# One weight sum of the Strassen-like gate/up sets, written in place

## The chip, the cores and the metric

The kernel runs on one core of a Trainium2 chip. The metric is the device time of one execution, in microseconds, lower is better. Before the change it is 1257.70 us, the median of three runs (1257.69 to 1257.84). One further execution was taken with the hardware profiler; everything below that is called a row of the profile or of the trace comes from that execution.

## The reference

The reference is a decoder trunk of two layers on 256 tokens of width 1024 in float32. Each layer adds, one after the other, half a SwiGLU feed-forward network (FFN), a token mixer (differential attention in layer 0, a Mamba-2 mixer in layer 1), a cross-attention into 256 memory tokens, and half of a second FFN:

```
def swiglu(h, w_gate, w_up, w_down):
    return (jax.nn.silu(h @ w_gate) * (h @ w_up)) @ w_down
...
    h = h + 0.5 * swiglu(rmsnorm(h, ffn1_norm[i]), ffn1_w_gate[i], ffn1_w_up[i], ffn1_w_down[i])
```

There are so four FFNs, and each has a gate and an up matrix of 1024 x 2816 and a down matrix of 2816 x 1024. What matters here is `h @ w_gate` and `h @ w_up`.

## The kernel before, in words

**Three products for one.** To reach float32 accuracy every operand is cut into two fp32r parts, high and low, and every product is made as three TensorE products: high x high, high x low, low x high (`mm3`, L261 to L264). The left operand is kept in its two parts. The weights come from memory in float32 and are cut on the chip: a granule (`Gran`, L205) is a piece of 128 x 1024 elements of a weight buffer; its `split` casts the high part on ACT (L224, tile `whi`) and then subtracts on DVE to get the low part (L225, tile `wlo`). There are four `whi` and four `wlo` buffers (pool `hp`), so the cast of a granule has to wait until TensorE is done with the granule four places ahead of it.

**Seven products for eight.** For blocks of 512 hidden columns, gate and up are made together by a Strassen-like scheme (`seven`, L361) that takes seven half-size products where the plain way takes eight. The weights of one such set are four tiles of 512 x 512: B11 and B21 (the upper and lower half of the rows of the up matrix), B12 and B22 (the same of the gate matrix). Beside products with B11, B22 and B21 themselves, the scheme needs products with four sums: x1 = B11 + B12, x2 = x1 + B22, x3 = B12 + B22, and x4 = x2 + B21. Signs sit on the left operand. There are 15 such sets: blocks 2, 3 and 4 of the first FFN and blocks 1 to 4 of the other three. Cross-attention calls `seven` twice more, with another order of the products.

**How the sums are made.** `Sum.load` (L186 to L203) makes a sum when its first granule is cut. With `into` unset it takes a weight buffer of its own and DVE writes the sum there (L192 and L203); with `"dve"` DVE writes it onto the left summand's buffer (L194 and L203); with `"dma"` the second summand is added onto the left summand's buffer by two accumulating DMAs that POOL issues (L199). In the gate/up sets x1 has a buffer of its own, x2 is written onto x1's, x4 is added by DMA onto x2's, and x3 by DMA onto B12's. So x3's DMA can start only when x1 has read B12, and x2's sum only when both granules of x1 are cut.

**Buffers.** All weight tiles, loaded or summed, come from one pool of nine buffers of 128 x 2048 floats (`wp`, L63). Loads are issued on SP's queue (L161, L176); each waits there until the buffer that it takes is free.

**The order of the work.** In the gate/up sets the products come in the order B11, x1, x2, B22, x3, B21, x4 (the argument `(1, 0, 3, 2, 5, 4, 6)` at L887; two granules each, six TensorE products per granule). Between them `share` (L395) puts granules of other work, called hosts here (twelve TensorE products each): the rest of gate and up, and the down matrix. `counts` (L870, L873) say how many before each of the seven: in the later three FFNs blocks 1 and 3 have one host before B11, blocks 2 and 4 have none, and in all of them one host stands before x1 and one before x2. `use` and `ready` (L231 to L241) write the split of a granule into the program two granules ahead of its products, so in program order B11's two splits and a host's stand before x1's sum and x1's splits. But program order is not queue order: only a few stretches are written with the order of the queues by hand (`manual_schedule`, L249 and L255). Elsewhere a planner in the framework places each instruction in its engine's queue as soon as, by its own estimates, what it needs is there. The queues themselves run in order.

Lines that the change and the prediction touch: L187 to L203 (`Sum.load`), L224 and L225 (`Gran.split`), L262 to L264 (`mm3`), L361 to L393 (`seven`), L843 (DVE, the end of an up block), L859 (DVE, low part of the hidden values, tile `hid_lo`), L887 (the call).

Of the kernel before, what the change touches and what calls it, by code (L numbers as in the profile page):

```python
# [57 lines left out]
def trunk(ctx, tc, a, out):  # L58
# [16 lines left out]
    def acc(name):  # L75
        return pacc.tile([P, 512], F32, name=name, tag="acc")
# [31 lines left out]
    class Pipe:  # L108
# [4 lines left out]
        def after(self, us, f):  # L113
            self.q.append((self.t + us, f))
# [146 lines left out]
    def mm3(o, lh, ll, rh, rl, start, stop, onto=False):  # L261
        nc.tensor.matmul(o, lhsT=lh, rhs=rh, start=start, stop=False, skip_group_check=onto)  # L262
        nc.tensor.matmul(o, lhsT=lh, rhs=rl, start=False, stop=False, skip_group_check=onto)  # L263
        nc.tensor.matmul(o, lhsT=ll, rhs=rh, start=False, stop=stop, skip_group_check=onto)  # L264
# [96 lines left out]
    def seven(b1, b2, x, mix, after, order=(0, 1, 2, 3, 5, 4, 6), second="dma"):  # L361

        b11, b21 = (W(b1[0], k, 4, b1[1], 512) for k in (0, 4))
        b12, b22 = (W(b2[0], k, 4, b2[1], 512) for k in (0, 4))
        x1 = Sum(b11, b12)
        x2 = Sum(x1, b22, second)
        x4 = Sum(x2, b21, "dma")
        x3 = Sum(b12, b22, "dma")
        banks = {}

        def a(t, h):
            return lambda k: tuple(v[:, t * P:(t + 1) * P] for v in pipe.need(x, 4 * h + k))

        def s(i):
            return lambda k: tuple(v[:, k * P:(k + 1) * P] for v in pipe.need(mix, i))
        plan = [(x1, s(0)), (b11, a(0, 0)), (b22, s(1)), (x2, s(2)), (b21, a(0, 1)), (x3, s(3)), (x4, a(1, 1))]
        out = []
        for i in order:
            w, lhs = plan[i]
            for k0 in (0, 2):  # L380
                def step(g, i=i, lhs=lhs, k0=k0):
                    if not k0:
                        banks[i] = banks[ONTO[i]] if i in ONTO else acc("seven")
                    for k in range(k0, k0 + 2):
                        lh, ll = lhs(k)
                        mm3(banks[i], lh, ll, g.hi[:, k - k0, :], g.lo[:, k - k0, :], k == 0 and i < 2, k == 3, onto=i in ONTO)
                        pipe.pe(0.68)
                    if k0:
                        for w in {0: (x2, x3), 3: (x4,)}.get(i, ()):
                            w.load()  # L390
                        after(i, banks)
                out.append((Gran(w.k0 + k0, 2, (w, 0, 512)), step))
        return out  # L393
# [388 lines left out]
    def ffn_hidden(nm, l, norm, fin, tail, extra=None):  # L782
# [103 lines left out]
        for c, k in counts.items():  # L886
            s = seven((wu, c * 512), (wg, c * 512), norm.x, norm.s, seven_fin(c), (1, 0, 3, 2, 5, 4, 6), "dve")  # L887
            steps += share(n[:sum(k)], s, k)
            n = n[sum(k):]
# [225 lines left out]
    def cross_attention(l, norm, kv, nxt):  # L1115
# [86 lines left out]
        wkv = a["xa_w_kv"][l]  # L1202
        q = [g for c in (2, 0) for g in columns(a["xa_w_q"][l], c * 256, norm, "xq", [q_fin(c), q_fin(c + 1)])]
        weave(share(q, seven((wkv, 1024), (wkv, 1536), kv.x, kv.s, mv_fin()), [2, 1, 1, 2, 1, 1, 0]))
        out_b(a["xa_w_o"][l], KT, ot, upd(1.0, nxt), (4, 0))

# [480 lines left out]
```

## Time and profile before

| | |
|---|---|
| median of three runs | 1257.70 us |
| the profiled execution, its own time | 1258.38 us |
| its span (first to last instruction) | 1256.6 us |
| mean granted TensorE clock | 0.999 |
| PE busy | 1247.1 us |
| weight loads of PE (PEld) | 1071.7 us |
| DVE busy | 1057.2 us |
| ACT busy | 873.5 us |
| POOL busy | 162.5 us |
| read from HBM | 271.72 MB, 218 GB/s over the span |

How to read it: times are in us from the span's start unless marked ns. PE is TensorE's products, DVE the vector engine, ACT the scalar engine, POOL GpSimd, SP the engine that issues most loads. A row of a timeline gives the start, the duration, the engine, the line, the operation, the output tile and what it is made from, the shape, a count where like instructions follow each other, and in brackets the idle time of the engine before it and what ended it. Successive instructions of an engine overlap a little: one may be listed as starting 0.08 us before the end of the one before. PE products overlap much more; the distance between the starts of two products is what PE needs for one, and an ended wait is counted as idle only past the modelled end of the product before. In the tables by stretch each engine has its busy time and, behind it, its instructions; then come the granted clock, DMA share and GB/s.

### The profile page before, as it was taken

The numbers are of one execution on the slowest core, as the hardware profiler recorded it, in microseconds if no ns is written. First come the engines' busy times: TensorE is split into PE (matmuls) and PEld (weight loads), VectorE is DVE, ScalarE is ACT, GpSimd is POOL, SyncE is SP. The second block draws the span as 40 slices with busy tenths as digits, with TensorE's granted clock in tenths as the row PEclk, the third lists the DMA queues.
The fourth block names the chain that finished last, engine by engine and source line by source line (L and its number), as shares of the span: only waits on it lengthen the run. The fifth ranks groups of instructions, "written<-read, shape, count | busy, mean of one in ns | idle before, by whom it ended". The sixth has DMA issues, their size and how long they took to land.

```text
span 1256.6 us, 18186 instructions
## 1 busy us (share of the span) xinstructions
PE 1247.1 (99%) x6751; PEld 1071.7 (85%) x6751; DVE 1057.2 (84%) x1451; ACT 873.5 (70%) x1388; POOL 162.5 (13%) x139
## 2 busy tenths in 40 slices
PE   9999999999999999999999999999999999999997
PEld 7888888788998888888888889999998898888886
DVE  6998787887787999887998976798898887898886
ACT  6676764686676776767776756777876775877772
POOL 1101102101101111110111000022233100011100
PEclk9999999999999999999999999999999999999999
DMA  9989976445776688987879977665636586489961
GB/s 330 301 255 259 314 256 208 137 165 170 222 214 170 165 252 260 293 246 234 240 198 268 311 247 221 192 193 168 201 134 185 169 246 182 157 251 256 258 190 34
DMA packets 161195, 275.03 MB, mean 219 GB/s; under 512 B 7209, under 2 KB 43730, under 8 KB 161106
## 3 DMA queue, kind: packets, MB, share of 16 engines
q1 hardware_dynamic: 137744, 229.75, 53.4%
q0 software_dynamic: 19744, 38.28, 17.7%
q10 hardware_dynamic: 3618, 5.84, 1.4%
q8 instruction: 53, 0.87, 0.3%
q14 instruction: 36, 0.29, 0.1%
HBM read 271.72 MB, written 2.13 MB: 218 GB/s over the span
## 4 chain that ended last, share of the span: by engine, by line
PE 94%; DMA 2%; DVE 2%; ACT 2%; issue 1%; POOLq 0%; POOL 0%; SPq 0%; ACTq 0%; DVEq 0%
PE out L262 9%; PE out L264 9%; PE out L263 9%; PE seven L263 8%; PE seven L262 8%; PE seven L264 8%; PE htp L855 1%; PE up L263 1%; PE up L264 1%; PE up L262 1%; PE xs L264 1%; PE xs L262 1%; PE xq L263 1%; PE xq L264 1%; PE xs L263 1%; PE xq L262 1%
## 5 line engine op out<-in xcount | busy, mean ns | idle before, releaser
L225 DVE TENSOR_TENSOR wlo<-w,whi 128x1024 fp32r<-128x1024 f32 (+2 forms) x532 | 639.4, 1220 | 134.6 <-ACT whi L224 126.8
L224 ACT CAST whi<-w 128x1024 fp32r<-128x1024 f32 (+2 forms) x534 | 551.0, 1039 | 245.2 <-PE out L264 84.0
L262 PE MATMUL out<-whi,hid_hi 128*128 128x512 f32 x336 | 132.3, 394 | 0.0
L264 PE MATMUL out<-whi,hid_lo 128*128 128x512 f32 x336 | 131.0, 390 | 0.0
L263 PE MATMUL out<-wlo,hid_hi 128*128 128x512 f32 x336 | 130.8, 389 | 0.0
L263 PE MATMUL seven<-wlo,s_hi 128*128 128x512 f32 x272 | 106.0, 390 | 0.6 <-DVE wlo L225 0.6
L262 PE MATMUL seven<-whi,s_hi 128*128 128x512 f32 x272 | 106.2, 390 | 0.0
L264 PE MATMUL seven<-whi,s_lo 128*128 128x512 f32 x272 | 105.9, 389 | 0.0
L199 POOL DMA_DIRECT2D w<-in_ffn_w_up_dram x30 | 36.7, 1268 | 346.6 <-DVE wlo L225 339.5
L203 DVE TENSOR_TENSOR w<-w 128x2048 f32<-128x2048 f32 x32 | 73.2, 2287 | 2.0 <-DMA w<-in_ffn_w_gate_dram 1.5
L264 PEld LDWEIGHTS out<-whi,hid_lo 128*128 128x128 f32 x336 | 63.1, 188 | 13.4
L263 PEld LDWEIGHTS out<-wlo,hid_hi 128*128 128x128 f32 x336 | 63.1, 188 | 12.6
L262 PEld LDWEIGHTS out<-whi,hid_hi 128*128 128x128 f32 x336 | 63.1, 188 | 12.5
L262 PE MATMUL seven<-whi,xh 128*128 128x512 f32 x180 | 70.5, 392 | 0.0
L264 PE MATMUL seven<-whi,xl 128*128 128x512 f32 x180 | 70.1, 389 | 0.0
L263 PE MATMUL seven<-wlo,xh 128*128 128x512 f32 x180 | 70.0, 389 | 0.0
L263 PEld LDWEIGHTS seven<-wlo,s_hi 128*128 128x128 f32 x272 | 51.1, 188 | 11.4 <-DVE wlo L225 1.0
L264 PEld LDWEIGHTS seven<-whi,s_lo 128*128 128x128 f32 x272 | 51.1, 188 | 10.7
L262 PEld LDWEIGHTS seven<-whi,s_hi 128*128 128x128 f32 x272 | 51.1, 188 | 10.4
L199 POOL DMA_DIRECT2D w<-in_ffn_w_gate_dram x30 | 36.9, 1467 | 176.2 <-DVE xst L1146 62.3
L264 PEld LDWEIGHTS seven<-whi,xl 128*128 128x128 f32 x180 | 33.8, 188 | 7.1
L262 PEld LDWEIGHTS seven<-whi,xh 128*128 128x128 f32 x180 | 33.8, 188 | 6.8
(395 smaller groups left out, 3013.7 us busy)
## 6 DMA issues: line engine op xcount, KB each, us to landing
w<-in_ffn_w_up_dram SPq DMA_DIRECT2D x40, 1024.0 KB, 7.8
w<-in_ffn_w_down_dram SPq DMA_DIRECT2D x40, 1024.0 KB, 9.3
w<-in_ffn_w_gate_dram SPq DMA_DIRECT2D x38, 1024.0 KB, 8.9
w<-in_ssd_w_in_dram SPq DMA_DIRECT2D x24, 1024.0 KB, 5.4
w<-in_xa_w_kv_dram SPq DMA_DIRECT2D x16, 1024.0 KB, 6.4
w<-in_ffn_w_gate_dram POOLq DMA_DIRECT2D x30, 512.0 KB, 9.7
w<-in_ffn_w_up_dram POOLq DMA_DIRECT2D x30, 512.0 KB, 7.2
w<-in_da_w_in_dram SPq DMA_DIRECT2D x12, 1024.0 KB, 5.2
```

The costliest lines, as they stand in the source:

```text
L199: nc.gpsimd.dma_start(self.t[:, k:k + 2, :], w.src[r0:r0 + 2 * P, w.c0:w.c0 + w.n] .rearrange("(k p) c -> p k c", p=P), accum_op=ALU.add)
L203: nc.vector.tensor_tensor(self.t, self.l.t, w.t, op=ALU.add)
L224: nc.scalar.copy(hv, src)
L225: self.eng.tensor_tensor(self.lo[:, :, o:o + n], src, hv.bitcast(F32), op=ALU.subtract)
L262: nc.tensor.matmul(o, lhsT=lh, rhs=rh, start=start, stop=False, skip_group_check=onto)
L263: nc.tensor.matmul(o, lhsT=lh, rhs=rl, start=False, stop=False, skip_group_check=onto)
L264: nc.tensor.matmul(o, lhsT=ll, rhs=rh, start=False, stop=stop, skip_group_check=onto)
L855: nc.tensor.transpose(tp[:, j, t * P:(t + 1) * P], us[t][:, (i + j) * P:(i + j + 1) * P], ident)
```

## The change

One line of `seven` changes. In the calls whose order of products begins with B11 (the 15 gate/up sets, not the two of cross-attention), x1 is made with `into="dve"`: DVE writes B11 + B12 onto B11's buffer, and x1 takes no buffer of its own. B11's two granules have to be cut before that. x2 and x4 go on to be made on the buffer that x1 is in, which is now B11's.

```
-        x1 = Sum(b11, b12)
+        x1 = Sum(b11, b12, "dve" if order[0] == 1 else None)
         x2 = Sum(x1, b22, second)
         x4 = Sum(x2, b21, "dma")
         x3 = Sum(b12, b22, "dma")
```

More of the change, by code (lines that the diff above doesn't have):

```diff
@@ L364, in seven @@
         b12, b22 = (W(b2[0], k, 4, b2[1], 512) for k in (0, 4))
-        x1 = Sum(b11, b12)
+        x1 = Sum(b11, b12, "dve" if order[0] == 1 else None)
         x2 = Sum(x1, b22, second)
```

## The prediction

> **What bounds the kernel now.** I read the page first, then the waits of PE and SP, then the timeline of single sets.
>
> ```profile
> span 1256.6 us, 18186 instructions
> PE 1247.1 (99%) x6751; PEld 1071.7 (85%) x6751; DVE 1057.2 (84%) x1451; ACT 873.5 (70%) x1388; POOL 162.5 (13%) x139
> ...
> L203 DVE TENSOR_TENSOR w<-w 128x2048 f32<-128x2048 f32 x32 | 73.2, 2287 | 2.0 <-DMA w<-in_ffn_w_gate_dram 1.5
> ```
>
> PE is busy for all but 9.5 us of the span. The whole list of what PE itself waited for is three lines long:
>
> ```profile
> PE warm L597 <- DVE warm L99: 1.5, 1, 1.5
> PE seven L263 <- DVE wlo L225: 0.6, 1, 0.6
> PE acs L1285 <- PE mk L264: 0.2, 1, 0.2
> ```
>
> So PE sets the time, and a change of buffers can gain no more than these waits, while any new wait of PE is paid in full. SP's loads do wait for buffers, long and often:
>
> ```profile
> SPq L161 <- DVE wlo L225: 790.4, 158, 15.8
> ```
>
> but none of that reaches PE: no DMA stands in PE's list. The second line of that list, the only wait of PE inside the sets, turns out to be the key, because it belongs to the one set in which x1's sum already stands behind B11's split.
>
> **Where x1's sum stands now.** The next rows are the timeline of DVE and POOL around the last set (block 4) of layer 0's second FFN.
>
> ```profile
> 499.49 2.28 DVE L203 TENSOR_TENSOR w<-w 128x2048 f32<-128x2048 f32 x1
> 502.13 2.45 POOL L199 DMA_DIRECT2D w<-in_ffn_w_gate_dram  x2 [0.89 <-DVE w L203]
> ...
> 520.92 2.54 DVE L225 TENSOR_TENSOR wlo<-w,whi 128x1024 fp32r<-128x1024 f32 x2 [0.92 <-ACT whi L224]
> 523.38 0.75 DVE L843 SCALAR_TENSOR_TENSOR p<-seven,rcol,p 128x512 f32<-128x512 f32 x1
> 524.04 2.35 DVE L225 TENSOR_TENSOR wlo<-w,whi 128x1024 fp32r<-128x1024 f32 x2
> 526.42 2.29 DVE L203 TENSOR_TENSOR w<-w 128x2048 f32<-128x2048 f32 x1
> 528.63 1.28 DVE L859 TENSOR_TENSOR hid_lo<-htp,hid_hi 128x512 fp32r<-128x512 f32 x2
> 529.83 4.62 DVE L225 TENSOR_TENSOR wlo<-w,whi 128x1024 fp32r<-128x1024 f32 x4
> ```
>
> The add at 499.49 is x1 of this set: the pair of accumulating DMAs onto B12 (x3, from the gate matrix) follows it at once. It stands 21 us ahead of B11's second split, which is the first of the pair at 520.92 (the second is the host's). The planner could put it there, in a roomy place, because it needed only B11, B12 and a free buffer. The pair at 524.04 is x1's split, the add at 526.42 is x2's sum, and of the four at 529.83 the second and third are x2's split. PE at the same place:
>
> ```profile
> 525.25 0.39 PE L263 MATMUL out<-wlo,hid_hi 128*128 128x512 f32 x1
> ...
> 534.08 0.39 PE L262 MATMUL seven<-whi,s_hi 128*128 128x512 f32 x1
> 534.30 0.39 PE L263 MATMUL seven<-wlo,s_hi 128*128 128x512 f32 x1
> ```
>
> 525.25 is the first product with the host's low part and 534.30 the first with x2's.
>
> **The change, part by part.** *Removed:* one buffer per set between x1's sum and the end of B11's split. Nothing but SP's loads feels it, and PE waits for none of them, so its gain is between 0 and, if the wait of 0.6 in the set's row above were a buffer's, 0.9; I take 0. *The add itself* is as long onto its own operand as onto another buffer: 2.28 at 499.49 (own buffer), 2.29 at 526.42 (in place). DVE's sum of busy time does not change. *Moved:* the add now reads and overwrites what B11's two casts and subtractions read, so it goes behind B11's second subtraction. It needs no further wait there (that subtraction has waited for the cast), but behind it on DVE stand the host's split, the end of the previous block (L843) and x1's split; on ACT the casts of x1, and behind them in order every cast of the set; on POOL x3's two DMAs. On SP the load that takes B11's buffer is let go later, and one load more has a buffer earlier.
>
> The question is what room DVE has in the place to which the add goes. In blocks 2 and 4 of the later three FFNs no host stands before B11. These six stretches, from B11's second split to x2's second (the first, the second and the last of six, and their sum):
>
> ```profile
> 450.58:463.00 12.42, 12.42 (x60) 10.35 (x59) 12.30 (x12) 9.43 (x11) 0.79 (x1) 1.00 0.54 185
> 520.92:533.30 12.38, 12.38 (x60) 10.34 (x59) 12.26 (x12) 9.43 (x11) 0.75 (x1) 1.00 0.87 319
> ...
> 1191.74:1204.10 12.36, 12.36 (x60) 10.32 (x59) 12.24 (x12) 9.42 (x11) 0.72 (x1) 1.00 1.00 370
> sum 74.33, PE 74.33 PEld 62.00 DVE 73.59 ACT 56.56 POOL 4.57; mean PE 12.39 PEld 10.33 DVE 12.26 ACT 9.43 POOL 0.76
> ```
>
> DVE (the third busy time) has 12.26 of 12.39 us in use, 99%. Another add takes 528.63 - 526.42 = 2.21 us of its time. What DVE can give is its lead over PE. In the row at 529.83 the four splits are (4.62 - 1.22) / 3 = 1.13 apart, so x2's first ends at 529.83 + 1.13 + 1.22 = 532.18, and PE reads it at 534.30: a lead of 2.12. Three ends of the cost, by the order in which the planner lays the queue:
> - Everything slides by 2.21 and nothing else opens: x2's split is 2.21 - 2.12 = 0.09 late. This is the low end.
> - After x2's sum, ACT has to cast and DVE has to wait for it. Now the two `hid_lo` and the host's split fill that time. If x2's sum comes out behind them, as the last of what is ready, the hand-over lies bare. The first FFN's block 2 (rows below) shows such a bare one at 1.17. Then x2's split is 0.09 + 1.17 = 1.26 late.
> - If the host's split also goes ahead of x1's sum, the hand-over at x1 is bare too: 2.43. This is the high end.
>
> In the first case the host's own split, pushed from 523.46 (520.92 + 2.54) by 2.21 to 525.67, also comes after 525.25, so that 0.4 is lost there instead. The trace has one set with this very order, block 2 of the first FFN (DVE, then PE):
>
> ```profile
> 46.22 2.29 DVE L203 TENSOR_TENSOR w<-w 128x2048 f32<-128x2048 f32 x1
> ...
> 53.20 2.28 DVE L203 TENSOR_TENSOR w<-w 128x2048 f32<-128x2048 f32 x1
> 56.66 2.36 DVE L225 TENSOR_TENSOR wlo<-w,whi 128x1024 fp32r<-128x1024 f32 x2 [1.17 <-ACT whi L224]
> ```
> ```profile
> 56.92 0.39 PE L262 MATMUL seven<-whi,s_hi 128*128 128x512 f32 x1
> 57.93 0.50 PE L263 MATMUL seven<-wlo,s_hi 128*128 128x512 f32 x1 [0.63 <-DVE wlo L225]
> 58.27 0.40 PE L264 MATMUL seven<-whi,s_lo 128*128 128x512 f32 x1
> ```
>
> Its sums are 7 us apart, x1's directly behind B11's and a host's split; and there PE waits for x2's low part. From start to start it takes 1.01 and 0.34 where 0.22 to 0.23 is usual (534.08 to 534.30): 0.8 + 0.1 = 0.9 lost. I take 1.1 per tight set, between this measured 0.9 and the worked 1.26: 6 x 1.1 = 6.6.
>
> The other nine sets. Block 2 of the first FFN has the new order already: 0. In the rest DVE has an idle stretch behind B11's split; these rows, of a block 1, a block 3 (with the host's split behind x2's sum) and block 4 of the first FFN, show it:
>
> ```profile
> 418.23 1.23 DVE L225 TENSOR_TENSOR wlo<-w,whi 128x1024 fp32r<-128x1024 f32 x1 [1.98 <-ACT whi L224]
> 490.03 2.59 DVE L225 TENSOR_TENSOR wlo<-w,whi 128x1024 fp32r<-128x1024 f32 x2 [1.05 <-ACT whi L224]
> 495.93 1.22 DVE L225 TENSOR_TENSOR wlo<-w,whi 128x1024 fp32r<-128x1024 f32 x1
> ...
> 128.94 1.23 DVE L225 TENSOR_TENSOR wlo<-w,whi 128x1024 fp32r<-128x1024 f32 x1 [1.05 <-ACT whi L224]
> ```
>
> Blocks 1 (three sets): 1.98 of 2.21 fit, 0.2 eats into a lead of some us: 0. Blocks 3 (three): 1.05 fit, 1.16 is left, so that the host's split behind x2's sum ends at 495.93 + 1.22 + 1.16 = 498.31; PE reads it at 498.05 (row below), 0.26 late at most; 0.1 taken each, 0.3. Of the first FFN, block 4 has the idle time of the last row, and block 3 has two hosts between x1 and x2 where the others have one: 0.
>
> ```profile
> 498.05 0.39 PE L263 MATMUL out<-wlo,hid_hi 128*128 128x512 f32 x1
> ```
>
> *x3's DMAs* move from 502.13 to about 524.4 + 0.4. Their transfers:
>
> ```profile
> DMA to landing us min/median/max: 5.7/7.4/13.8
> ...
> 544.96 0.39 PE L262 MATMUL seven<-whi,s_hi 128*128 128x512 f32 x1
> ```
>
> Both halves are issued within 2.45, by 527.2, and the second lands by 541.0 at worst. PE starts x3 at 544.96 and reads the low part of its second half seven products later, at 546.55; hand-over and subtraction (1.17 + 1.23) have to lie before, from 544.1. Free, by 3 us.
>
> Sum: 6.6 + 0.3 = 6.9, all on PE's path. The profiled execution took 1258.38 (span 1256.6 and 1.8 around it), so 1265.3; the median of the runs is 0.7 below that execution: 1257.7 + 6.9 = 1264.6.
>
> **The rivals.**
>
> *No change that can be measured.* A measurement of this kernel tells about 0.2%, 2.5 us, from no change. If the planner lets the host's split go first and puts `hid_lo` behind x2's sum, each tight set pays the low end, 0.1 to 0.4: 6 x 0.2 = 1.2, 1258.9. For it: DVE is idle 16% of the span, and the planner chooses by what is ready. Against: in 12.39 us there are only 0.13 to choose from, and the set at 46.22 lost 0.9. It decides below 0.4 per tight set.
>
> *Faster through the freed buffer.* SP waits 790 us for buffers; one more could start loads earlier. But PE's own waits bound the gain: 0.9 at 57.93 and 0.2, so 1256.6. [...] To be faster by over 2.5 us needs something that no row shows.
>
> *Much slower.* Both hand-overs bare in the six (2.43 each, 14.6) and one in the three blocks 3 (0.26 + 1.17, 4.3): 18.9, 1276.6; likewise if x3's second half took 17 us or more to land, when each further us would cost one per set. Nothing in the rows asks for it.
>
> **How the numbers follow.** The forecast (6.9, from 0.5 to 1.7 per tight set, 1261 to 1268) 0.57; no change 0.28; much slower 0.12; faster than 1255.2 0.03. So slower 0.69, same 0.28, faster 0.03. The range goes from 1257.6, which leaves out the faster case and a third of the no-change case at most, to 1273, which leaves out half of the much slower one. The prediction is 1264.6.
>
> **What would show it.** Right: in the tight sets x1's add stands between B11's split and x1's cast, PE has new waits for `wlo` at x2 or at the host before it, some 5 us in the list of PE's waits where 0.6 stood, and DVE's busy time stays at 1057. x3's DMAs come 20 us later, and SP's waits get shorter. Wrong, if the adds stand there and PE's list stays at three short lines: then the lead was larger than 2.12 or the planner repacked the stretch. Wrong in kind, if PE waits for a DMA, or if `L203` of x1 still stands 20 us ahead.

## The result and the profile after

The changed kernel takes 1276.65 us (median of four runs, 1276.12 to 1277.4); the kernel before, on the same chip, 1257.77 us. The ratio is 1.015, with a 95% interval from 1.0134 to 1.0166: slower by 18.9 us where 6.9 had been forecast. The profiled execution took 1276.47 us, with a span of 1274.7 us. From the page of the kernel after, its first lines and the engines' shares of the chain that ended last:

```profile
span 1274.7 us, 18198 instructions
PE 1254.1 (98%) x6751; PEld 1071.1 (84%) x6751; DVE 1057.0 (83%) x1451; ACT 867.9 (68%) x1388; POOL 162.2 (13%) x139
...
PE 84%; DVE 8%; ACT 4%; issue 2%; DMA 1%; ACTq 0%; POOLq 0%; POOL 0%; DVEq 0%
```

DVE does the same work in the same time (1057.0 against 1057.2), yet its share of the chain has risen from 2% to 8%. The first two lines of PE's waits after (the others, 1.9 us in all, are not in the sets), with total, count and longest:

```profile
PE seven L263 <- DVE wlo L225: 7.6, 10, 0.8
PE seven L262 <- ACT whi L224: 4.2, 2, 3.4
```

Two things stand there. The first line is many small waits for `wlo`, as foretold, though larger. The second holds one wait of 3.4 us, which nobody had foretold. On SP the line that the prediction showed has grown (790.4 before):

```profile
SPq L161 <- DVE wlo L225: 854.1, 162, 15.4
```

Other lines of SP's list have shrunk (L176 behind `wlo` from 89.1 to 43.1); all lines of L161 and L176 together come to 1092 against 1078 before, so the loads wait hardly longer, and not shorter.

**Where the 18 us lie.** I matched the products of the two traces and took the difference of their start times along the run. It grows in steps, and only in or beside the gate/up sets:

| place | lost, us |
|---|---|
| six tight sets (blocks 2 and 4 of the later three FFNs), 0.3 at the host before x1 and 1.2 at x2 in each | 9.0 |
| three blocks 3 of the later FFNs, 1.1 in each | 3.3 |
| blocks 1 of the later FFNs | 0 |
| first FFN, of it block 4 +1.1 and its earlier part -0.3 | 0.8 |
| one stop in the last set of layer 1's first FFN, beside that set's own 1.5 | 5.1 |
| the rest | -0.2 |

They come to 18.0; the difference at the last products is 18.1, as is that of the two profiled spans (the medians are 18.9 apart).

**A tight set.** DVE in block 4 of layer 0's second FFN, the set that the prediction showed at 520.92 to 529.83:

```profile
524.36 1.23 DVE L225 TENSOR_TENSOR wlo<-w,whi 128x1024 fp32r<-128x1024 f32 x1 [0.92 <-ACT whi L224]
525.62 2.29 DVE L203 TENSOR_TENSOR w<-w 128x2048 f32<-128x2048 f32 x1
527.83 1.22 DVE L225 TENSOR_TENSOR wlo<-w,whi 128x1024 fp32r<-128x1024 f32 x1
528.97 0.74 DVE L843 SCALAR_TENSOR_TENSOR p<-seven,rcol,p 128x512 f32<-128x512 f32 x1
529.63 2.35 DVE L225 TENSOR_TENSOR wlo<-w,whi 128x1024 fp32r<-128x1024 f32 x2
532.08 1.29 DVE L859 TENSOR_TENSOR hid_lo<-htp,hid_hi 128x512 fp32r<-128x512 f32 x2
533.29 1.22 DVE L225 TENSOR_TENSOR wlo<-w,whi 128x1024 fp32r<-128x1024 f32 x1
534.42 2.28 DVE L203 TENSOR_TENSOR w<-w 128x2048 f32<-128x2048 f32 x1
537.87 3.50 DVE L225 TENSOR_TENSOR wlo<-w,whi 128x1024 fp32r<-128x1024 f32 x3 [1.17 <-ACT whi L224]
```

x1's add (525.62) is directly behind B11's second split and ahead of the host's (527.83). x2's sum (534.42) has slid behind both `hid_lo` and the next host's split, so that nothing is left for DVE while ACT casts: it idles for 1.17. PE at the same place:

```profile
529.10 0.50 PE L263 MATMUL out<-wlo,hid_hi 128*128 128x512 f32 x1
...
537.89 0.49 PE L262 MATMUL seven<-whi,s_hi 128*128 128x512 f32 x1
539.15 0.50 PE L263 MATMUL seven<-wlo,s_hi 128*128 128x512 f32 x1 [0.77 <-DVE wlo L225]
539.49 0.39 PE L264 MATMUL seven<-whi,s_lo 128*128 128x512 f32 x1
```

x2's first low product starts 1.26 after the product before it, and the next one 0.34 later, where 0.23 is usual: 1.14 lost. The bracket shows 0.77 of it, because a wait is counted only past the end of the product before. So PE's list (7.6) understates the loss, and the distances of the starts have to be read. The host's low part (529.10) costs 0.3 more by the matched starts.

**A block 3.** DVE in the block 3 before it; then ACT's cast of x1's first granule in the kernel after, and the same cast in the kernel before:

```profile
490.09 1.22 DVE L225 TENSOR_TENSOR wlo<-w,whi 128x1024 fp32r<-128x1024 f32 x1
491.22 2.29 DVE L203 TENSOR_TENSOR w<-w 128x2048 f32<-128x2048 f32 x1
494.70 1.22 DVE L225 TENSOR_TENSOR wlo<-w,whi 128x1024 fp32r<-128x1024 f32 x1 [1.19 <-ACT whi L224]
...
499.31 2.28 DVE L203 TENSOR_TENSOR w<-w 128x2048 f32<-128x2048 f32 x1
502.76 2.36 DVE L225 TENSOR_TENSOR wlo<-w,whi 128x1024 fp32r<-128x1024 f32 x2 [1.17 <-ACT whi L224]
```
```profile
493.62 1.05 ACT L224 CAST whi<-w 128x1024 fp32r<-128x1024 f32 x1 [4.00 <-DVE w L203]
```
```profile
488.94 1.05 ACT L224 CAST whi<-w 128x1024 fp32r<-128x1024 f32 x1 [1.66 <-PE out L264]
```

x1's add (491.22) stands here behind the split of the host before x1 (490.09), and the next split, 494.70, is x1's own. Both hand-overs lie bare, 1.19 behind x1's sum and 1.17 behind x2's. Before the change x1's cast at 488.94 had only to wait until PE had left the buffer four places ahead (a host's, hence `out`), and DVE's idle 1.05 before 490.03 was the time of this cast. Now the cast waits for the add (493.62), so that the add does not fill the idle time but comes ahead of it.

**The stop.** PE in the last set of layer 1's first FFN, then ACT and POOL at the same time, then ACT in the kernel before at this place (`my` is the tile into which a part of the memory tokens is loaded):

```profile
717.24 0.39 PE L264 MATMUL out<-whi,hid_lo 128*128 128x512 f32 x1
721.04 0.50 PE L262 MATMUL seven<-whi,s_hi 128*128 128x512 f32 x1 [3.42 <-ACT whi L224]
722.30 0.80 PE L263 MATMUL seven<-wlo,s_hi 128*128 128x512 f32 x1 [0.76 <-DVE wlo L225]
722.89 0.63 PE L264 MATMUL seven<-whi,s_lo 128*128 128x512 f32 x1
723.32 0.63 PE L262 MATMUL seven<-whi,s_hi 128*128 128x512 f32 x1
```
```profile
711.53 0.33 ACTq L1074 DMA_DIRECT2D my<-memt  x1
...
714.94 0.59 ACT L827 COPY p<-seven 128x512 f32<-128x512 f32 x1 [2.78 <-PE seven L264]
719.15 0.91 ACT L457 ACTIVATE mh<-my,cols 128x256 fp32r<-128x256 f32 x2 [3.62 <-DMA my<-memt]
719.96 3.87 ACT L224 CAST whi<-w 128x1024 fp32r<-128x1024 f32 x4
```
```profile
707.90 2.47 POOL L199 DMA_DIRECT2D w<-in_ffn_w_gate_dram  x2 [21.45 <-DVE w L203]
```
```profile
704.42 0.33 ACTq L1074 DMA_DIRECT2D my<-memt  x1
...
713.95 0.91 ACT L457 ACTIVATE mh<-my,cols 128x256 fp32r<-128x256 f32 x2
```

The rows show ACT's queue running in order. In it the cut of a memory token (`mh`, L457), work of the coming cross-attention, stands ahead of x2's cast and waits 3.62 us for its load; x2's cast, whose sum was done at 716.32, starts only at 719.96, and PE stands still from 717.24 to 721.04.

The load that the cut waits for is issued at 711.53 and there by 719.15, 7.6 us later (the three behind it land 9.6 to 10.2 after their issue). ACT comes to the cut when its copy ends at 715.53, 4.0 us after the issue. In the kernel before, the cut stands behind x2's casts, 9.5 us lie between issue (704.42) and cut (713.95), and nothing waits. The load has not become late: at 708 PE's products are 7.9 us behind those of before, and 704.42 + 7.9 would be 712.3. It is the cut that has come forward in ACT's queue, to a place that ACT reaches before x2's sum is done. x3's moved pair (707.90) is under way with these loads; its halves land at 717.45 and 722.01.

### The profile page after: what moved, and what is told of

Same layout as the page of the kernel before. It is cut to its first block, busy times and chain, and to the rows that moved or that the text cites. A ratio compares the mean times of both kernels' runs of the same rounds, so it can differ in the third digit from the quotient of the medians.

```text
span 1274.7 us, 18198 instructions
## 1 busy us (share of the span) xinstructions
PE 1254.1 (98%) x6751; PEld 1071.1 (84%) x6751; DVE 1057.0 (83%) x1451; ACT 867.9 (68%) x1388; POOL 162.2 (13%) x139
## 4 chain that ended last, share of the span: by engine, by line
PE 84%; DVE 8%; ACT 4%; issue 2%; DMA 1%; ACTq 0%; POOLq 0%; POOL 0%; DVEq 0%
PE out L262 8%; PE out L264 8%; PE out L263 8%; PE seven L263 7%; PE seven L264 7%; PE seven L262 6%; DVE wlo L225 3%; DVE w L203 3%; ACT whi L224 3%; PE xs L264 2%; PE xs L262 2%; PE xs L263 2%; PE up L263 1%; PE up L264 1%; PE up L262 1%
## 5 line engine op out<-in xcount | busy, mean ns | idle before, releaser
L827 ACT COPY p<-seven 128x512 f32<-128x512 f32 x45 | 26.3, 585 | 31.0 <-PE seven L264 31.0
L466 POOL TENSOR_TENSOR rcol<-msq,neghalf 128x2 f32<-128x2 f32 x8 | 6.7, 838 | 267.1 <-DVE msq L464 267.1
```

The lines of the kernel that those rows point to most:

```text
L466: nc.gpsimd.tensor_tensor(c[:, :n], m[:, :n], neghalf[:, :n], op=ALU.pow)
L827: nc.scalar.copy(t[i], b[i])
```

## The experiments

My theory after the two traces was: the buffer is harmless; the place to which the add is forced costs PE the lead that DVE had, and the stop is a collision on ACT that can be taken away by itself. The rivals were that the shift of buffers and of loads costs the time, that x3's moved DMAs do, and that the add is too long a piece rather than in a wrong place.

**1. The place alone.** The kernel before, with x1 in a buffer of its own, but with the add held behind B11's second subtraction:

```
+                if self.late:
+                    with tc.issue_after(self.l.cut.ins):
+                        nc.vector.tensor_tensor(self.t, self.l.t, w.t, op=ALU.add)
...
-        x1 = Sum(b11, b12)
+        x1 = Sum(b11, b12, late=order[0] == 1)
```

> The kernel before, with x1 still in a buffer of its own, but its add held on DVE behind the subtraction of B11's second granule, as in the changed kernel. Theory A (the place of the add on DVE is what costs: it takes 2.2 us of a stretch in which DVE is 99% busy, and ACT's cast of x1 and x2 then wait for sums with nothing to fill DVE): nearly all of the loss comes back without any change of buffers, 1257.7 + 13 = 1271, up to 1277 if the collision at 717 us comes too. Theory B (the buffer costs: B11's buffer is held until x4 is done, loads and the accumulating DMAs get in each other's way): the buffers are those of before, so 1257.7 to 1259.

Measured: 1269.97 us (1269.74 to 1270.18), ratio 1.0097 (1.0082 to 1.0112). PE's waits in it (its lines are numbered five higher):

```profile
PE seven L268 <- DVE wlo L230: 7.9, 11, 0.8
```

The waits for `wlo` are there in full with the buffer as it was (7.9 against 7.6; 0.6 of the 7.9 is the wait that the kernel before has in the first FFN's block 2). No stop is there: the memory tokens' loads take 7.7 us and more here too, but their first cut stands behind x2's cast, at 719.96, 9.7 us after the issue at 710.29. So 12.2 of the 18.9 us come with the place of the add, and none of that needs the other buffer. x3's DMAs move along with the add here too, but PE waits for no DMA.

**2. The tight sets alone.** In place only in the six tight sets:

```
-        x1 = Sum(b11, b12, "dve" if order[0] == 1 else None)
+        x1 = Sum(b11, b12, first)
...
+            ..., "dve" if c in (2, 4) and norm is not first_norm else None)
```

> The change in six sets alone, blocks 2 and 4 of the later three FFNs. Theory A: each loses about 0.3 at the host before x1 and 1.2 at x2, as in the changed kernel's trace: 6 x 1.5 = 9, so 1266.8, or 1272 if the 5 us at block 4 of layer 1's first FFN come too; no wait of PE in blocks 1 and 3. Theory B, a cost of each in-place set alike (18.9 / 14 per moved set): 6 x 1.35 = 8, 1265.8, with PE's waits for loads and not for the low part; told from A by what PE waits for.

Measured: 1273.22 us (1272.47 to 1274.37), ratio 1.0124 (1.0109 to 1.0139). PE's waits:

```profile
PE seven L263 <- DVE wlo L225: 5.2, 7, 0.8
PE seven L262 <- ACT whi L224: 3.6, 2, 3.4
```

Of the other sets only the first FFN's block 2 has such a wait, the 0.6 of the kernel before, and the stop came here too, at 714. It is 15.4 us over the kernel before, for the six sets and the stop: 14.1 by the table, and 1.3 because the granted clock was 0.50 for 6.8 us behind the stop and not for 3.4 (last section). It is 3.4 below the kernel after, for the blocks 3 and the first FFN (4.1 by the table).

**3. The stop alone.** The kernel after, with the loads of the memory tokens issued at the end of block 3 (675.0 to 676.6) and no longer within block 4 (711.5 to 712.9):

```
-            ... else {12: kvs[1].fetch, 8: kvs[1].prep})
+            ... else {6: kvs[1].fetch, 8: kvs[1].prep})
```

> The changed kernel, with the four loads of the stored memory tokens (tile my) issued one block earlier, behind block 3 instead of behind block 4's sixth product. Theory A1 (the 3.8 us stop of PE at 717 us, and the eight products at 0.43 us behind it, come from ACT's queue: it stands at mh, which waits for the load my that landed 10 us after its issue beside x3's moved DMAs): the stop and the slow products go, 1276.6 - 5.1 = 1271.5, and 1.5 are lost in this set as in the others. Theory A2 (the stop is x2's sum and its cast being late on DVE, and mh only happens to stand there): 1276.6.

Measured: 1271.56 us (1271.33 to 1271.82), ratio 1.011 (1.0095 to 1.0125), 5.1 below the kernel after, as expected. ACT at the same place:

```profile
712.45 0.92 ACT L457 ACTIVATE mh<-my,cols 128x256 fp32r<-128x256 f32 x2
...
716.82 4.90 ACT L224 CAST whi<-w 128x1024 fp32r<-128x1024 f32 x5 [0.48 <-DVE w L203]
```

The cut of the memory tokens still stands ahead of x2's cast, but no longer waits for a load, x2's cast waits only for its sum, and the long wait is gone from PE's list, while the line of 7.6 us for `wlo` stays as it was.

**4 to 6. What the freed buffer is worth, and a longer lead.** The fourth takes the freed buffer away (`wp` from nine buffers to eight). The fifth spends it on a fifth pair of `whi` and `wlo` as well, so that granules can be cut one place further ahead. The sixth does the same to the kernel before, as a control.

```
-    wp = ctx.enter_context(tc.tile_pool(name="wp", bufs=9))
-    hp = ctx.enter_context(tc.tile_pool(name="hp", bufs=4))
+    wp = ctx.enter_context(tc.tile_pool(name="wp", bufs=8))
+    hp = ctx.enter_context(tc.tile_pool(name="hp", bufs=5))
```

> The changed kernel with eight weight buffers where there were nine, so that the buffer that the change frees is taken away again. Theory A (no load of weights reaches PE): 1276.6, within 1.5. Theory B (loads matter): later loads, and a loss of more than 3: 1280 or above.

Measured: 1278.48 us (1278.33 to 1278.57), ratio 1.0165 (1.0148 to 1.0182): 1.8 over the kernel after, a little more than the theory allowed, by new waits of at most 1.0 us each.

> The changed kernel with eight weight buffers, and the room that the freed one took given to a fifth pair of buffers for the cut weights (whi, wlo), so that a cast may run one granule further ahead of its products. Theory A (a lack of lead: x2's split had 2.1 us, and sum and hand-over take 2.2 + 1.2): one granule more of 1.36 us gives 3.5, so the waits of 1.0 at x2 and of 0.2 at the host nearly go, in blocks 3 as well; with 1.8 for eight buffers and 2 to 4 for the stop at mh 1260 to 1265. Theory C (DVE is simply out of time there, and whatever lead there is gets eaten up): 1.3 to 1.5 per tight set stay, 1275 to 1278.

Measured: 1259.43 us (1259.23 to 1259.61), ratio 1.0012 (1.0003 to 1.0022), just below the expected range. PE's list has four lines, 3.6 us in all; none of them is for `wlo`, and the stop is gone. DVE in the tight set:

```profile
519.78 2.29 DVE L203 TENSOR_TENSOR w<-w 128x2048 f32<-128x2048 f32 x1
...
527.20 2.29 DVE L203 TENSOR_TENSOR w<-w 128x2048 f32<-128x2048 f32 x1
529.40 1.28 DVE L859 TENSOR_TENSOR hid_lo<-htp,hid_hi 128x512 fp32r<-128x512 f32 x2
```

x1's add is as long as before and still directly behind B11's second split, but it stands 5.8 us earlier (3.7 of them are the time by which the kernel after is behind at that point), and x2's sum comes ahead of `hid_lo`, which fills the hand-over. With one place more of lead the late add costs almost nothing.

> The control to the run with five pairs: the kernel before, x1 in a buffer of its own, with eight weight buffers and five pairs of cut ones. Theory A: DVE had lead enough but for the 0.9 at block 2 of the first FFN, and PE waited for no load: 1256.8 to 1260, the upper end if nine buffers were needed for five tiles per set.

Measured: 1273.35 us (1271.84 to 1275.29), ratio 1.0125 (1.011 to 1.014). My expectation missed by 13 us. DVE's waits tell why:

```profile
DVE w L203 <- DMA w<-in_ffn_w_gate_dram: 19.7, 7, 4.6
```

With x1 in a buffer of its own, eight buffers are too few: x1's add waits for a load, at worst 4.6 us, and behind it on DVE waits everything else; PE's largest entry is 7.5 us of waiting for `gs`, which DVE makes behind such an add. So the freed buffer is a real resource. In the changed kernel it can be given up for 1.8 us; in the kernel before, giving it up (with a fifth pair in exchange) cost 15.6. The kernel before with eight buffers and four pairs was not run, so how much of that belongs to the buffer alone is not separated from the pairs.

**7 and 8. Both sums in halves.** The kernel after, with each DVE sum made as two adds of 1024 columns, and the same in the kernel before:

```
-                nc.vector.tensor_tensor(self.t, self.l.t, w.t, op=ALU.add)
+                for k in (0, 2):
+                    nc.vector.tensor_tensor(self.t[:, k:k + 2, :], self.l.t[:, k:k + 2, :], w.t[:, k:k + 2, :], op=ALU.add)
```

> The changed kernel with both DVE sums of a set, x1's and x2's, each made as two adds of 128 x 1024 instead of one of 128 x 2048. DVE's work grows by 30 x about 0.06 us. Theory A (half of the loss is the hand-over, in which the cast waits for a whole sum): the first half is done 1.1 us earlier and its cast starts then, the second half can go between; x2's wait of 1.0 goes and the host's of 0.2 may, in blocks 2 to 4 alike: 1276.6 - 9 x 1.1 = 1266.7, with the 5 us at 717 us still in it; 1262 without. Theory C (DVE out of time): 1276 to 1278.

Measured: 1257.41 us (1257.14 to 1257.71), ratio 0.9997 (0.9988 to 1.0007): all 19 us are back, more than I had expected. PE's list has two waits left, 1.5 at the start and 0.2. DVE in the tight set (lines are numbered one higher):

```profile
517.79 1.21 DVE L226 TENSOR_TENSOR wlo<-w,whi 128x1024 fp32r<-128x1024 f32 x1
519.04 1.23 DVE L204 TENSOR_TENSOR w<-w 128x1024 f32<-128x1024 f32 x1
520.18 2.36 DVE L226 TENSOR_TENSOR wlo<-w,whi 128x1024 fp32r<-128x1024 f32 x2
522.45 0.75 DVE L844 SCALAR_TENSOR_TENSOR p<-seven,rcol,p 128x512 f32<-128x512 f32 x1
523.11 1.22 DVE L204 TENSOR_TENSOR w<-w 128x1024 f32<-128x1024 f32 x1
```

The first half of x1 needs only B11's first granule, so it goes between B11's two splits (519.04), ahead of the tight stretch. The second half comes at 523.11, behind the host's split, and ACT meanwhile casts what the first half has made, so that no hand-over is bare. In the kernel after, DVE was idle for 17% of the span, but in the stretch where PE's waits arose it had 12.26 of 12.39 us in use before the change.

> The control to the halves: the kernel before with both sums as two adds each. Theory A: the only loss of this kind before was 0.9 at block 2 of the first FFN, which goes: 1256.8. Theory C: 1257.7 or a little above.

Measured: 1257.17 us (1256.9 to 1257.36), ratio 0.9993 (0.9984 to 1.0003). The wait in the first FFN's block 2 (0.6 in the list of before) is gone, but the time can't be told from the kernel before. Halves are thus no gain by themselves; they pay only where the sum is late.

**9 and 10. One sum in halves.** The kernel after with x1 alone, then with x2 alone, in halves:

```
+                step = 2 if isinstance(self.l, W) else 4      # 9: x1;  10: isinstance(self.l, Sum), x2
+                for k in range(0, 4, step):
+                    nc.vector.tensor_tensor(self.t[:, k:k + step, :], self.l.t[:, k:k + step, :], w.t[:, k:k + step, :], op=ALU.add)
```

> The changed kernel with x1's sum alone made as two adds of 128 x 1024; x2's stays one. Theory D (what the halves cure is the place: x1's first half needs only B11's first granule cut and so leaves the tight stretch, 1.2 us of DVE's time come back, and the hand-over at x1 is short): most of the loss goes, 1258 to 1262. Theory E (what they cure is the hand-over at x2, where the waits of 1.0 stand): 1272 to 1276, the wait at x2 stays.

Measured: 1265.21 us (1264.82 to 1266.3), ratio 1.006 (1.0045 to 1.0075), between the ranges of both theories.

> The changed kernel with x2's sum alone made as two adds of 128 x 1024; x1's stays one. Theory D: x1's 2.2 us still lie in the tight stretch and the host's wait of 0.2 stays; x2's wait falls by the 1.1 of its second half at most: 1262 to 1268. Theory E: as good as both, 1257.5 to 1259.

Measured: 1262.32 us (1261.61 to 1262.68), ratio 1.0034 (1.0021 to 1.0047). PE's waits for `wlo` in its list are 3.1 us in the ninth, six waits of at most 0.5, and a single one of 0.2 in the tenth.

Neither cut does it alone. By the start times of the products, x1 in halves takes away the 0.3 at the host and leaves 0.8 at x2 in each tight set; x2 in halves leaves the 0.3 at the host and 0.2 at x2 (0.45 in one set). The stop is gone in both. A half of x1 is short enough for the host's split to be in time, and halves of x2 cover its hand-over: while ACT casts the first half, DVE adds the second. Both suspected causes are there, side by side. Against the kernel after without the stop (1271.56) the two cuts save 6.4 and 9.2, together 14.2, so they nearly add. The ninth also loses 0.9 in each of two blocks 1, at 426 and 1102, where neither the kernel after nor the seventh loses anything; why is not shown.

**11 and 12. Halves and the freed buffer.** The seventh with eight buffers, and with eight and a fifth pair (the two edits shown above put together).

> The changed kernel with both sums in halves and eight weight buffers in place of nine. If the freed buffer is really free (theory A: no load of weights reaches PE once x1 has no buffer of its own): 1257.4 plus at most the 1.8 that eight buffers cost in the changed kernel, so 1257 to 1259.5. If the planner needs nine (as the kernel before did, which lost 15 with eight and five pairs): 1262 or above.

Measured: 1257.66 us (1257.07 to 1258.82), ratio 0.9997 (0.9988 to 1.0007).

> The changed kernel with both sums in halves, eight weight buffers, and the room of the ninth as a fifth pair of cut weights. PE has hardly a wait left in the run with halves, so theory A gives nothing more: 1257 to 1259.5. If a lack of lead still hides in PE's pace: below 1256.

Measured: 1258.73 us (1258.21 to 1260.12), ratio 1.0009 (1.0 to 1.0018). With halves the buffer is really free: it can be given up at no measurable cost. That is 8 KB less in each partition (2048 floats), at the time of before. A fifth pair brings nothing more. No version was measurably faster than the kernel before.

## Why the prediction was wrong, point by point

The table has 18.0 us where 6.9 stood. Of the 11.1 between them, 5.1 are the stop, which the prediction put at nothing, 3.0 the blocks 3, 2.4 the tight sets and 0.8 the first FFN, less the 0.2 of the rest.

- *PE sets the time, and any new wait of PE is paid in full.* Right: DVE's busy time stayed (1057.0 against 1057.2), and the shift of PE's products, 18.1 at the last ones, is that of the span. The stop cost 1.5 beyond its length.
- *x1's add must leave its roomy place and go directly behind B11's second split.* Right in the tight sets (525.62; in the blocks 3 the host's split still comes between), and the first experiment shows that this alone makes 12.2 us.
- *The lead over PE in the tight sets is 2.12, and the add spends it.* Right as mechanism; a fifth pair, which lengthens the lead, takes the loss away (1259.43). *1.1 per tight set* was the mis-sized term: it measured 1.5. The step that failed is the word "instead" at the host's split: "0.4 is lost there instead". The add goes ahead of the host's split and x2's sum goes behind `hid_lo` and the next host's split, in the same set. So the 0.3 at the host comes on top of the 1.2 at x2 (1.26 had been worked out for x2 alone). Six sets: 9.0 where 6.6 stood.
- *Blocks 3 lose 0.1 each.* Wrong: 1.1 each, 3.3 where 0.3 stood. The step that failed is "1.05 fit". The 1.05 us of idle time that I wanted to fill with the add is the time in which DVE waits for the cast of x1 itself, and after the change this cast can only begin when the add is done, so nothing of the add fits there. And I carried the bare hand-over of 1.17 only into the tight sets, although it depends on the sum's place in the queue and not on how full the stretch is. The rows show it bare at both sums.
- *Blocks 1 lose nothing.* Right. There the idle 1.98 lies ahead of the host's split, for a cast that needs no sum, and the add fits in (417.00 to 419.28). *The first FFN loses nothing:* wrong for block 4, which lost 1.1 for the reason of the blocks 3; right for block 2.
- *x3's DMAs are free by 3 us.* For x3 itself right: PE never waits for it. But the sum has no term for other work that the planner moves when the sums come later. It drew the cut of a memory token ahead of x2's late cast on ACT, with a load under way that took 7.6 us when only 4.0 were left: the stop, 5.1 us. The third experiment shows that it goes when the load is issued earlier, with the cut still ahead; in the first, the cut stands behind x2's cast and there is no stop, although x3's pair moved and the loads were slow there too. So it takes both, the order on ACT and a load that is not there yet. Whether x3's pair is what makes these loads slow stays open: in the kernel before two of them took 3.5 and 3.8 us with no such pair just issued, and one, 3.1 us behind x4's pair, took 8.8; in the third experiment they took 7.0 to 12.0, from 1.1 us behind block 3's pair for x3. No run moves the pair alone.
- *SP's waits get shorter.* Not so: 1092 against 1078 for its loads. PE's list has no DMA in it either way.
- *The much slower rival* named 18.9, which is the measured number, but by another road: it had 2.43 in each tight set, where 1.5 was found, and no stop. That the sums agree is chance. What was right in it are the bare hand-overs in the blocks 3.

The kernel with only the late add (1269.97) and the kernel after without the stop (1271.56) differ by 1.6 us. The starts of the products put this into the six tight sets, which lose 7.7 us together in the first and 9.4 in the second. In the first the add starts 1.14 us after the start of B11's second split (525.00 behind 523.86), in the kernel after 1.26 (525.62 behind 524.36), and the host's split comes ahead of `hid_lo`. Why an add in a buffer of its own starts that much sooner is not shown.

## What to carry to other kernels

A sum written in place saves a buffer and adds an order: the add may start only when the last reader of its operand is done. So look where in the queue it stood, not how long it takes, and when it is forced into a full stretch count every hand-over to another engine there as bare (1.17 to 1.19 us each here), several in one stretch as a sum and not as alternatives. Idle time of the engine can take the sum only if what it waits for does not itself need the sum. And look at what else the planner may draw into the new gaps: on a queue that runs in order, one instruction that waits for a load holds all behind it (on ACT 3.62 us here, with x2's sum done at 716.32 and its cast at 719.96). Then cut the piece at the granularity of its readers and its users before giving the change up: in halves the same change cost nothing (1257.41 against 1257.77), and the buffer was free (1257.66).

## What the runs showed of the hardware

The stop of PE cost more than its length, 5.1 us for 3.6. After the 3.8 us without a product (717.24 to 721.04) the products are 0.43 us apart (722.89 to 723.32) where 0.23 is usual. The kernel after, then the kernel of the tight sets, each in the stretch of the slow products, with PE, PEld, DVE, ACT and POOL busy, the granted clock, the DMA share and GB/s:

```profile
722.23:725.64 3.41, 3.34 (x8) 2.69 (x9) 3.41 (x4) 2.40 (x3) 2.44 (x2) 0.50 0.35 38
```
```profile
718.42:725.25 6.83, 6.16 (x15) 4.86 (x16) 5.25 (x5) 4.71 (x7) 2.44 (x2) 0.50 0.63 115
```

The granted clock is 0.50 for 3.4 us in the first and for 6.8 in the second, after stops of the same length (714.00 to 717.83 there), and back at 1.00 behind them (means of the profiled executions: 0.998 and 0.996, against 0.999 before). Of the 5.1 us the stop itself is 3.8 - 0.23 = 3.6; the other 1.5 are this slow stretch, and in the second kernel it costs 1.3 more. In the sixth experiment two shorter stops had such a sequel as well, 3.4 us at 0.50 each (mean 0.997): the products before and behind them start 2.8 and 2.6 us apart (438.19 to 441.02, 1117.64 to 1120.23). One of 2.2 us there (618.47 to 620.70) had none, nor had the stops of about 1 us at each x2. What sets the length of the slow stretch is not shown.

The add of 1024 columns takes 1.22 us and that of 2048 columns 2.29: two halves cost 2.44, some 0.15 more by durations, but two directly behind each other overlap (2.35 for x2's two halves in the tenth experiment). DVE's busy time in the seventh is 1059.2 against 1057.0, so the cut into halves is nearly free on DVE.
